# Rotating an 8192 x 8192 float32 array: which outputs of the last but one macro tile go through 32x32 blocks, and who makes their copies

## The chip, the cores and the metric

The kernel runs on one core of a Trainium2 chip. The metric is the device time of one execution in microseconds (us), as the median of several; before the change it is 1263.31 us (three runs, 1263.1 to 1263.37).

## The reference

`reference(x, k)` returns `np.rot90(x, k)` for x of 8192 x 8192 float32 and k = 1: out[8191 - c, r] = x[r, c]. Nothing is calculated; 268.44 MB are read, turned by a quarter, and 268.44 MB are written.

## The kernel before

**Tiles.** x is cut into 16 macro tiles (numbered kk = 0 to 15) of R = 1024 rows by W = 4096 columns. A macro tile is loaded in T = 8 loads of 128 rows each (2 MB; load t of macro tile kk is called kk.t, and has the number m = 8 kk + t) and stored in J = 8 outputs of 512 columns of x each, over all its 1024 rows (2 MB; output j is called kk.j, number n = 8 kk + j). So there are 128 loads and 128 stores, and the 8 outputs of a macro tile need all of its 8 loads. In macro tile 15 alone the outputs are cut otherwise: the first four are halves of two columns of outputs (`END`, `wide`), so that the end does not wait for all rows.

**On-chip buffers.** `bufs` has two landing buffers (LAND) and three output buffers (OUTS); `ring` holds one macro tile less one chunk (SLOTS = T * J - 1). Each load is a row of 8 chunks of 128 x 512. VectorE reads a landed load, reverses each chunk and puts it into its slots of the ring (L337). Macro tiles of even and odd number lay their chunks out crosswise (`slot`), so that load kk.t goes into exactly the slots that output (kk-1).t has been read from. Therefore VectorE waits, ahead of load m = n + 8, until output n has been taken out of the ring.

**Two ways for an output.** `by_pe(kk)` lists the outputs of a macro tile that TensorE turns: it transposes 128x128 pieces into PSUM (L376), and ScalarE copies them out into an output buffer (L415), in three parts. All outputs of macro tiles 0 and 15 go that way; of macro tiles 1 to 13 outputs 0 and 4 (`BY_PE`); of macro tile 14 outputs 0, 4 and 7. The other outputs are *moved*: VectorE puts their chunks into the ring with a STREAM_TRANSPOSE, which turns 32x32 blocks, in place of a plain copy, and afterwards whole quadrants (32 partitions) have to be copied into an output buffer, 16 copies of 32x1024 for an output (`pairs`, `moves`). VectorE makes the first BY_DVE = 2 of them (L319), GpSimd the next BY_POOL = 9 (L294), ScalarE the last 5 (L405).

**Order and waits.** Every engine runs its own list, written out by hand, in order.
- SyncE issues the loads (L256); load m waits (`taken`) until VectorE has put the load two before it, m - 2, wholly into the ring.
- VectorE, for each load m: first its copies for output m - 8 if that is moved; then it waits for load m to land, then for output m - 8 to be out of the ring (`s_pool`, or `s_half` for an output of TensorE), then the pieces of the load.
- GpSimd, for each moved output: it waits for a free output buffer (`room_for`: the store three outputs earlier has landed), and makes 9 copies; ahead of the eighth it waits for ScalarE's copies, ahead of the ninth for VectorE's. So its count says that all 16 copies are done.
- ScalarE, for each output in order: its copies, or the parts out of PSUM; then, for a moved output, the wait for GpSimd's count; then it issues the store (L425). For output 7 it first takes a corner piece out of PSUM (L398).
- TensorE fills two PSUM halves in turn; the third part of an output reuses the half of the first, once ScalarE has emptied it. The last transposition of an output's first part waits for a free output buffer.

`pieces` says in how many instructions VectorE takes a load into the ring; `split` joins chunks that a regular pattern can describe.

Of the kernel before, what the change touches and what calls it, by code (L numbers as in the profile page):

```python
# [13 lines left out]
J = W // (G * P)  # L14
# [5 lines left out]
SLOTS = T * J - 1  # L20

Q = 32
BY_DVE = 2
BY_POOL = 9
BY_PE = [0, 4]

# [33 lines left out]
def kernel(tc: tile.TileContext, x: bass.AP, k: bass.AP, out: bass.AP):  # L60
# [7 lines left out]
    KK = len(macros)  # L68
# [11 lines left out]
    outs = [(*o, [(j, g * P) for j in reversed(o[2]) for g in range(G)]) for o in outs]  # L80

    def by_pe(kk):
        return list(range(J)) if kk in (0, KK - 1) else BY_PE + [J - 1] * (kk == KK - 2)

    def in_quadrants(kk, j):
        return j not in by_pe(kk)
# [29 lines left out]
    with tc.tile_critical():  # L116
# [72 lines left out]
        def split(js):  # L189
            while js:  # L190
                n = max(n for n in range(1, len(js) + 1) if strides(js[:n], 1))
                yield js[:n]
                js = js[n:]
# [3 lines left out]
        for m in range(n_load):  # L197
            kk, t = divmod(m, T)
            here = by_pe(kk)
            rest = [j for j in range(J) if j not in here]  # L200
            if kk == KK - 1:
                got = [here] if t < T - 1 else [here[:wide], here[wide:-1], here[-1:]]
            elif t < T - 1:
                got = [here[: len(BY_PE)], rest, here[len(BY_PE) :]]
                if kk == 0:
                    got = [here]
            else:
                inner = [j for j in here if 0 < j < J - 1]
                got = [here[:1], [J - 1], [j for j in rest if j < J - 1], inner]
            got = [part for js in got for part in split(js)]  # L210
            pieces[m] = got
            for js in got:
                done += 1
                for j in js:
                    rev[m, j] = done
# [16 lines left out]
        def moves(n, share):  # L232
            kk, ts, (j,), _ = outs[n]
            rows = len(ts) * P
            places = [slot(kk, t, j) for t in ts if (t, j) != (T - 1, J - 1)]
            ((step, tiles),) = strides(places, CH)
            for a, q in share:
                yield (
                    at(
                        bufs[out_buf(n)][q * Q : q * Q + Q, :],  # L240
                        a * Q,
                        [[rows, G], [P, tiles], [1, Q]],
                    ),
                    at(
                        ring[a * Q : a * Q + Q, :],
                        places[0] * CH + q * Q,
                        [[P, G], [step, tiles], [1, Q]],
                    ),
                )
# [10 lines left out]
        def turned_in(n):  # L260
            kk, _, (j,), _ = outs[n]
            return rev[kk * T + T - 1 - (j == J - 1), j]
# [7 lines left out]
        with nc.Block() as block:  # L270

            @block.gpsimd
            def _(e):
# [12 lines left out]
                for n, (kk, _, js, _) in enumerate(outs):  # L286
                    if moved[n]:
                        room_for(wait, n)
                        wait(s_rev, turned_in(n))
                        others = {BY_POOL - 2: s_act, BY_POOL - 1: s_dve}  # L290
                        for c, (to, of) in enumerate(moves(n, pairs[BY_DVE : BY_DVE + BY_POOL])):
                            if c in others:
# [16 lines left out]
            def _(e):  # L309
                wait = once(e)  # L310
                for m in range(n_load):
# [3 lines left out]
                    if n >= 0 and moved[n]:  # L315
                        room_for(wait, n)
                        wait(s_rev, turned_in(n))
                        for to, of in moves(n, pairs[:BY_DVE]):
                            i = e.tensor_copy(out=to, in_=of)  # L319
# [66 lines left out]
            def _(e):  # L386
# [3 lines left out]
                for n, (kk, ts, js, blocks) in enumerate(outs):  # L390
# [11 lines left out]
                    if moved[n]:  # L402
                        wait(s_rev, turned_in(n))
                        for to, of in moves(n, pairs[BY_DVE + BY_POOL :]):
                            i = e.copy(to, of)  # L405
# [60 lines left out]
```

## Time and profile before

| What | Value |
|---|---|
| median of three runs | 1263.31 us |
| profiled execution, own time | 1262.84 us |
| its span in the profile | 1261.0 us |
| VectorE busy | 714.8 us, 466 instructions |
| ScalarE busy | 600.8 us, 559 instructions |
| GpSimd busy | 848.2 us, 753 instructions |
| TensorE busy (matmul) | 314.3 us, 1492 instructions |
| HBM traffic | 268.44 MB read, 268.44 MB written |

The profile is of one execution. Times of its rows count from the start of the span; the execution's own time is 1.84 us longer than the span. In the rows PE is TensorE, PEld its weight loads, DVE VectorE, ACT ScalarE, POOL GpSimd, SP SyncE; a small q behind the name marks the queue on which an engine issues transfers. A row names the source line, the operation and what it writes and reads (out<-in), the count, and the time. In brackets stands how long the engine was idle before it, and what ended that idle time. DMA share is the mean busy share of the 16 DMA engines, GB/s what they moved.

### The profile page before, as it was taken

To read this page: it belongs to the slowest core of one execution; us is meant where nothing else is said; L and a number is where in the kernel's file an instruction comes from. 1 tells how busy PE (TensorE), PEld (TensorE's weight loads), DVE (VectorE), ACT (ScalarE), POOL (GpSimd) and SP (SyncE) were. 2 spreads that over 40 slices of the span, in tenths; PEclk is the share of its full clock that TensorE was granted. 3 is DMA by queue.
4 is the path that set the end of the run, shared out by engine and by line. 5 is a ranking of instruction groups with operands and counts; after the bars stand their busy time and mean duration, and the time that the engine had idled before them with its cause. 6 is when DMAs were issued, how large, how long until landed. Compare 5 with 4: busy or idle time off the path is not lost.

```text
span 1261.0 us, 5364 instructions
## 1 busy us (share of the span) xinstructions
PE 314.3 (25%) x1492; PEld 255.1 (20%) x1492; DVE 714.8 (57%) x466; ACT 600.8 (48%) x559; POOL 848.2 (67%) x753
## 2 busy tenths in 40 slices
PE   1555122221122211132202322113221132211273
PEld 1444011211112110121201212012120121201163
DVE  3444765567656666666666665666556665564510
ACT  0344454454445544454445545454454544534564
POOL 0001887778877779777797777877678777788910
PEclk9986555555555555555555555555555555555587
DMA  9999999999999999999999999999999999999999
GB/s 398 417 432 429 427 430 430 428 431 429 428 431 429 429 431 429 429 430 430 428 429 431 429 428 431 429 429 430 428 430 431 429 430 430 429 429 430 388 423 384
DMA packets 36893, 537.21 MB, mean 426 GB/s; under 512 B 4096, under 2 KB 4096, under 8 KB 4096
## 3 DMA queue, kind: packets, MB, share of 16 engines
q10 hardware_dynamic: 18432, 268.44, 50.1%
q1 hardware_dynamic: 18432, 268.44, 49.9%
q8 instruction: 11, 0.18, 0.1%
q14 instruction: 18, 0.15, 0.0%
HBM read 268.44 MB, written 268.44 MB: 426 GB/s over the span
## 4 chain that ended last, share of the span: by engine, by line
DMA 72%; DVE 16%; POOL 5%; ACT 3%; issue 2%; PE 0%; ACTq 0%; SPq 0%; DVEq 0%; POOLq 0%
DMA buf<-in_x_dram 65%; DVE ring L337 16%; DMA out_dram<-buf 7%; POOL buf L294 5%; ACT buf L415 3%; PE ps L376 0%; ACTq L425 0%; DVE buf L319 0%; SPq L256 0%; DVEq L324 0%; SPq L461 0%; POOLq L161 0%; SPq L116 0%
## 5 line engine op out<-in xcount | busy, mean ns | idle before, releaser
L294 POOL COPY buf<-ring 32x1024 f32<-32x1024 f32 (+1 forms) x747 | 847.5, 1135 | 353.9 <-DMA out_dram<-buf 301.1
L405 ACT COPY buf<-ring 32x1024 f32<-32x1024 f32 (+1 forms) x415 | 425.2, 1025 | 314.9 <-POOL buf L294 261.2
L376 PE MATMUL ps<-head,ring 128*128 128x128 f32 x1432 | 301.5, 382 | 927.6 <-DVE ring L337 413.3
L376 PEld LDWEIGHTS ps<-head,ring 128*128 128x128 f32 x1432 | 242.3, 198 | 986.6 <-DVE ring L337 426.3
L337 DVE COPY ring<-buf 128x1024 f32<-128x1024 f32 (+3 forms) x152 | 135.9, 895 | 498.8 <-DMA buf<-in_x_dram 433.2
L337 DVE STREAM_TRANSPOSE ring<-buf 128x3072 f32<-128x3072 f32 (+2 forms) x133 | 367.0, 2771 | 0.0
L415 ACT COPY buf<-ps 128x2048 f32<-128x2048 f32 (+4 forms) x127 | 165.5, 1370 | 241.4 <-PE ps L376 167.4
L319 DVE COPY buf<-ring 32x1024 f32<-32x1024 f32 x166 | 222.4, 1340 | 1.1
L398 ACT COPY buf<-ps 128x512 f32<-128x512 f32 x15 | 8.8, 586 | 86.1 <-POOL buf L294 80.4
L362 PE MATMUL ps<-head,buf 128*128 128x128 f32 x60 | 15.9, 421 | 0.0
L362 PEld LDWEIGHTS ps<-head,buf 128*128 128x128 f32 x60 | 13.1, 230 | 0.0
L332 DVE COPY buf<-buf 128x512 f32<-128x512 f32 x15 | 6.4, 427 | 0.5
L389 ACT ACT_TABLE_LOAD x1 | 1.3, 1283 | 0.9 <-SPq L116 0.9
L274 POOL MEMSET head<- 128x128 f32 x1 | 0.2, 204 | 0.5 <-SPq L116 0.5
L276 POOL TENSOR_SCALAR_AFFINE_SELECT head<-head 128x128 f32<-128x128 f32 x1 | 0.3, 292 | 0.2 <-POOL head L274 0.2
L447 POOL MEMSET const-float32-0.0<- 128x1 f32 x1 | 0.1, 98 | 0.2 <-issue 0.2
L389 ACT COPY head<-head 128x1 f32<-128x1 f32 x1 | 0.2, 192 | 0.0
L447 POOL MEMSET const-uint8-127<- 128x1 uint8 x1 | 0.1, 101 | 0.0
L447 POOL MEMSET const-bfloat16-1.0<- 128x1 bf16 x1 | 0.1, 100 | 0.0
L447 POOL MEMSET const-float32-1.0<- 128x1 f32 x1 | 0.1, 98 | 0.0
## 6 DMA issues: line engine op xcount, KB each, us to landing
buf<-in_x_dram SPq DMA_DIRECT2D x128, 2048.0 KB, 15.4
out_dram<-buf ACTq DMA_DIRECT2D x128, 2048.0 KB, 17.5
```

The costliest lines, as they stand in the source:

```text
L276: e.affine_select(out=ident, in_=ident, compare_op=mybir.AluOpType.not_equal, fill=1.0, base=0, pattern=[[-1, P]], channel_multiplier=1,). ...
L294: i = e.tensor_copy(out=to, in_=of)
L319: i = e.tensor_copy(out=to, in_=of)
L332: e.tensor_copy(out=at(bufs[b][:], 0, [[CH, 1], [1, CH]]), in_=landed(b, js)).then_inc(s_rev, 1)
L337: turn(out=chunk(kk, t, js), in_=landed(b, js)).then_inc(s_rev, 1)
L362: i = e.transpose(corner[:, g * P : g * P + P], bufs[load_buf(m)][:, g * P : g * P + P], ident,)
L376: i = e.transpose(ps[h][:, to : to + P], chunk(kk, t, [j])[:, 0, off : off + P], ident,)
L389: e.copy(scratch, ident[:, :1])
L398: e.copy(at(bufs[b][:], rows - P, [[rows, G], [1, P]]), at(corner, 0, [[P, G], [1, P]]),).then_inc(s_freed, 1)
L405: i = e.copy(to, of)
L415: e.copy(at(bufs[b][:], cols[0], [[rows, deep], [1, run]]), at(ps[h][:], 0, [[run, deep], [1, run]]),).then_inc(s_ev, 1)
L447: nc = _bacc.Bacc("TRN2", target_bir_lowering=False, num_devices=1)
```

## The change

```diff
-BY_DVE = 2
+BY_DVE = 1
 BY_POOL = 9
...
     def by_pe(kk):
-        return list(range(J)) if kk in (0, KK - 1) else BY_PE + [J - 1] * (kk == KK - 2)
+        if kk in (0, KK - 1):
+            return list(range(J))
+        return BY_PE if kk < KK - 2 else [*range(0, J, 2), J - 1]
...
             elif t < T - 1:
-                got = [here[: len(BY_PE)], rest, here[len(BY_PE) :]]
-                if kk == 0:
-                    got = [here]
+                got = [here, rest]
```

First, for every moved output of the whole kernel, VectorE makes one of the 16 quadrant copies instead of two, GpSimd still nine (each shifted by one quadrant pair), ScalarE six instead of five.

Second, in macro tile 14 TensorE turns outputs 0, 2, 4, 6 and 7 (before: 0, 4, 7), and only 1, 3 and 5 are moved (before: 1, 2, 3, 5, 6). So the number of moved outputs falls from 83 to 81.

Third, VectorE takes the loads 14.0 to 14.6 into the ring as a copy of chunks 0, 2, 4, 6, a copy of chunk 7 and a transposition of chunks 1, 3, 5; before it was a copy of 0 and 4, a transposition of 1, 2, 3, one of 5, 6, and a copy of 7. The last load, 14.7, keeps four instructions in the same order of kinds: chunk 0, chunk 7, the transposed ones, and the other plain ones. In the other macro tiles the pieces are the same as before.

## The prediction

> **What bounds the kernel now.** First I read the page: its span and the rate of the transfers in 40 equal slices.
>
> ```profile
> span 1261.0 us, 5364 instructions
> ...
> GB/s 398 417 432 429 427 430 430 428 431 429 428 431 429 429 431 429 429 430 430 428 429 431 429 428 431 429 429 430 428 430 431 429 430 430 429 429 430 388 423 384
> ```
>
> The DMA engines move about 429 GB/s whatever the other engines do. Where that holds, no engine's busy time matters; a change can win only where a slice falls off. Besides the start and the end only the 38th does, with 388. So next the view by windows, cut around that slice (window, length, busy time of PE, PEld, DVE, ACT, POOL with counts, granted clock, DMA share, GB/s).
>
> ```profile
> 180.00:1164.00 984.00, 206.20 (x845) 163.00 (x845) 599.81 (x403) 483.62 (x463) 761.67 (x678) 0.53 1.01 429
> 1164.00:1188.00 24.00, 7.19 (x30) 5.99 (x30) 13.79 (x7) 14.12 (x13) 21.63 (x16) 0.57 0.96 377
> 1188.00:1212.00 24.00, 7.96 (x47) 7.49 (x47) 8.03 (x4) 10.61 (x10) 14.66 (x12) 0.55 1.01 429
> 1212.00:1256.00 44.00, 26.52 (x226) 24.22 (x224) 2.69 (x3) 27.55 (x16) 0.00 (x0) 0.90 1.01 424
> ```
>
> The dip lies between stretches of 429 and costs 24 x (1 - 377/429) = **2.9 us**. The last 44 us are stores alone, at 424. Third, who is late in the dip: the timeline of VectorE, of ScalarE with its queue, and of SyncE's queue.
>
> ```profile
> 1163.87 3.14 DVE L337 COPY ring<-buf 128x4096 f32<-128x4096 f32 x1 [6.37 <-POOL buf L294]
> ...
> 1176.26 2.29 DVE L337 COPY ring<-buf 128x4096 f32<-128x4096 f32 x1 [6.37 <-POOL buf L294]
> ```
>
> ```profile
> 1137.78 0.55 ACTq L425 DMA_DIRECT2D out_dram<-buf  x1
> 1138.88 5.25 ACT L405 COPY buf<-ring 32x1024 f32<-32x1024 f32 x5 [1.13 <-DMA out_dram<-buf]
> 1151.27 0.55 ACTq L425 DMA_DIRECT2D out_dram<-buf  x1
> ...
> 1163.80 0.55 ACTq L425 DMA_DIRECT2D out_dram<-buf  x1
> ...
> 1176.19 0.55 ACTq L425 DMA_DIRECT2D out_dram<-buf  x1
> 1176.78 3.70 ACT L415 COPY buf<-ps 128x2048 f32<-128x2048 f32 x3 [7.13 <-POOL buf L294]
> 1180.51 0.56 ACTq L425 DMA_DIRECT2D out_dram<-buf  x1
> ```
>
> ```profile
> 1145.34 0.33 SPq L256 DMA_DIRECT2D buf<-in_x_dram  x1
> ```
>
> ```profile
> 1154.65 0.33 SPq L256 DMA_DIRECT2D buf<-in_x_dram  x1
> ```
>
> ```profile
> 1167.04 0.33 SPq L256 DMA_DIRECT2D buf<-in_x_dram  x1
> ```
>
> ```profile
> 1178.58 0.33 SPq L256 DMA_DIRECT2D buf<-in_x_dram  x1
> ```
>
> ScalarE's queue issues the stores 14.0 to 14.4 here; the moved ones 14.1, 14.2 and 14.3 come 12.5 and 12.4 us apart, one GpSimd output each. VectorE wants to take in the loads 15.2 and 15.3 and waits 6.37 us each time until GpSimd has finished 14.2 and 14.3; so SyncE's loads 15.4 and 15.5 (the last two rows) go out late. How late is seen from the times to landing, asked for each issue alone; the four loads 15.2 to 15.5, then the stores 14.0, 14.1, 14.2:
>
> ```profile
> DMA to landing us min/median/max: 16.7/16.7/16.7
> ```
>
> ```profile
> DMA to landing us min/median/max: 17.2/17.2/17.2
> ```
>
> ```profile
> DMA to landing us min/median/max: 12.7/12.7/12.7
> ```
>
> ```profile
> DMA to landing us min/median/max: 14.7/14.7/14.7
> ```
>
> ```profile
> DMA to landing us min/median/max: 20.6/20.6/20.6
> ```
>
> ```profile
> DMA to landing us min/median/max: 16.9/16.9/16.9
> ```
>
> ```profile
> DMA to landing us min/median/max: 14.1/14.1/14.1
> ```
>
> Landings are thus 15.2 at 1162.0, 15.3 at 1171.8, 15.4 at 1179.7, 15.5 at 1193.3; stores 14.0 at 1158.4, 14.1 at 1168.2, 14.2 at 1177.9. I call the **lead** of a transfer how long before the landing of its forerunner in the same direction it is issued. Load 15.3: 1162.0 - 1154.65 = 7.4 us; store 14.1: 1158.4 - 1151.27 = 7.1; both before the dip, so both without loss. Load 15.4: 4.8; store 14.2: 4.4; the rate just begins to fall. Load 15.5: 1.1; store 14.3: 1.7; that is the dip: one direction has nothing in flight, and between the landings of 15.4 and 15.5 lie 13.6 us, where a pair of load and store takes 4.194 MB / 429 GB/s = 9.8 us. So a lead of 7 is enough, one of 5 hardly, one of 1 is not.
>
> **The change part by part.** The prices, by shape:
>
> ```profile
> L294 POOL COPY buf<-ring 32x1024 f32<-32x1024 f32 x630 | 725.4, 1151 | 348.8 <-DMA out_dram<-buf 301.1 <-DVE buf L319 23.0
> L405 ACT COPY buf<-ring 32x1024 f32<-32x1024 f32 x350 | 364.5, 1041 | 314.0 <-POOL buf L294 261.2 <-DMA out_dram<-buf 48.8 <-ACT buf L415 0.7
> ...
> L319 DVE COPY buf<-ring 32x1024 f32<-32x1024 f32 x140 | 193.2, 1380 | 0.9
> ...
> L337 DVE COPY ring<-buf 128x1024 f32<-128x1024 f32 x99 | 82.2, 830 | 382.7 <-DMA buf<-in_x_dram 335.4 <-POOL buf L294 44.0 <-PE ps L376 3.3
> ...
> L337 DVE STREAM_TRANSPOSE ring<-buf 128x1536 f32<-128x1536 f32 x21 | 37.2, 1770 | 0.0
> L337 DVE COPY ring<-buf 128x4096 f32<-128x4096 f32 x14 | 34.5, 2462 | 59.5 <-DMA buf<-in_x_dram 41.2 <-POOL buf L294 17.0 <-PE ps L376 1.4
> ...
> L337 DVE STREAM_TRANSPOSE ring<-buf 128x1024 f32<-128x1024 f32 x21 | 25.2, 1201 | 0.0
> ```
>
> *One copy moves from VectorE to ScalarE* in each of 81 moved outputs. VectorE loses 1.38 us an output, ScalarE gains 1.04. Neither stands at the end of an output: GpSimd does, with 9 x 1.15 = 10.4 us against ScalarE's 6 x 1.04 = 6.2. Cost 0, under the cover of GpSimd. What if the cover goes is a rival below. GpSimd itself gets a little faster, as the chain of work shows in output 14.1:
>
> ```profile
> 1143.21 3.00 POOL buf L294
> 1146.25 1.40 POOL buf L294
> ...
> 1149.13 1.03 POOL buf L294
> ```
>
> Its copies take 1.03 us alone, 1.40 beside one of VectorE's quadrant copies (L319), 3.00 beside VectorE's 128x4096 copy. One L319 less is 0.37 us less for GpSimd per output; where GpSimd waits for the second VectorE copy (23.0 us in all in the first row), that goes too. In the 984 us at 429 GB/s this is worth 0, since the transfers are full.
>
> The Trainium skill ("Perfetto Trace Analysis", Optimizing Scalar/DVE Operations) says that a copy which VectorE can do in a performance mode is faster there, and should go to ScalarE only when VectorE is saturated. That speaks against this exchange, with VectorE busy 714.8 of 1261.0 us; the trace disagrees on the price, 1380 ns on VectorE and 1041 on ScalarE for the same shape. By the rule the sum would hold a loss in each output; by the rows it holds none.
>
> *Outputs 14.2 and 14.6 go to TensorE.* GpSimd loses 18 copies in macro tile 14, 20.7 us by the first row. TensorE gains 64 transpositions, ScalarE trades two sets of copies for two sets out of PSUM (3.70 us). *VectorE's intake of loads 14.0 to 14.6*: it loses transpositions of 1536 and 1024 (1.77 + 1.20) for one of 1536; its plain copy of 1024 becomes one of 2048, a shape that the trace lacks: between 0.83 (128x1024) and 2.46 us (128x4096), I take 1.3, being nearer to the smaller. Sum: between -1.20 and +0.43, taken -0.7 us per load. It stands between a load's landing and the issue of the load after next, so a lead grows by 0.7 or shrinks by 0.4: worth 0 at leads of 7.
>
> *Replay of macro tile 14*, with landings 9.8 us apart from the last one that is as before. GpSimd takes for a moved output seven copies of 1.03 with 0.04 between two (1143.21 + 3.00 to 1146.25), one of 3.00 and one of 1.40: 12.0 us (12.4 before). A store of TensorE's follows the one ahead by 4.3 us at least (1176.19 to 1180.51).
> - 14.1 (moved): its buffer comes free at 1138.9 as before, ready 1150.9, lead 7.5.
> - 14.2 (TensorE): ScalarE is free after that issue; 1155.3 in place of 1163.80, lead 12.9 in place of 4.4.
> - Load 15.2 landed at 1162.0; output 14.2 is out of the ring, so VectorE's 6.37 us wait becomes one for the landing. With 2.3 to 3.1 us of copy (the two VectorE rows), load 15.4 goes out at 1164.3 to 1165.1 in place of 1167.04: lead 6.7 to 7.5.
> - 14.3 (moved): buffer of 14.0 free at 1158.4, ready 1170.4 in place of 1176.19; lead on 14.2 (1178.0) 7.6.
> - Load 15.3 at 1171.8 finds 14.3 out; load 15.5 goes out at 1174.1 to 1174.9 in place of 1178.58: lead on 15.4 (now 1181.6) 6.7 to 7.5.
> - 14.4, 14.6 (TensorE) have leads of 13; 14.5 (moved) starts at 1178.0, is ready at 1190.0, lead 7.5 on 1197.5. Loads 15.6 and 15.7 follow as 15.5 does, with the same leads.
>
> No lead is left under 6.7. What is late next is then nothing but the transfers, up to the last load; there the stores 14.6 and 14.7 are still pending, as before, and cover macro tile 15's first outputs. The tail keeps its 44 us at 424.
>
> **Sum:** 1261.0 - 2.9 = 1258.1 us of span. The execution lies 1262.84 - 1261.0 = 1.84 over its span: 1259.9. The median of the runs, 1263.31, lies 0.47 over the profiled one: **1260.4 us**.
>
> **The rivals.**
> 1. *The dip shrinks only.* Leads of 6.7 to 7.5 lie between one that cost nothing (7.1) and one of 4.8, at which the rate fell; VectorE's 128x4096 copies still stretch a GpSimd copy to 3.00. The 2.9 us came with four late transfers (15.4, 15.5, 14.2, 14.3), 0.7 each; if each of the four loads 15.4 to 15.7 still loses half of that, 1.4 us stay: 1261.8. For it: no lead of these has more than 2 us to spare. Against: loads and stores with 7.4 and 7.1 ran at 429.
> 2. *It does not do what it should: the dip is no matter of late issues*, and stays: 1263.3. For it: stores alone run at 424 in the tail, so one direction could carry the whole rate. Against: in the tail several stores are queued, in the dip just one. The Trainium skill ("DMA: Bandwidth & Descriptors", Issuing engines are not separate DMA queues) says that transfers of all queues share the same 16 engines, and the queue of issue saves only issue time; by that rule alone a late load would leave its share to the store and 1263.3 would stand, and the 377 GB/s speak against it.
> 3. *Slower: ScalarE's sixth copy becomes what GpSimd waits for* ahead of its eighth. In the second of two consecutive moved outputs ScalarE starts 0.6 us after GpSimd (it issues the store first) and would end after 0.6 + 6 x 1.04 = 6.9 us; GpSimd's seven copies take 7 x 1.07 = 7.5 uncontended. It decides from 0.6 us more, and shows in the time only where leads fall under 5. At 0.1 us lost in each of the four such outputs of 13 macro tiles, 5.2 us: 1268.5. Against: the margin, and 348.8 us in which GpSimd is idle. The skill's rule on ScalarE above leads here too.
> 4. *More:* the steady stretch also rises by 1 GB/s (984/429 = 2.3 us): 1258.1. Against: it has no visible dip to fill.
>
> **How the numbers follow.** Forecast 0.66, with its own range 1259.7 to 1261.2; rival 1 0.18, rival 2 0.06, rival 3 0.06, rival 4 0.04. The range holds the forecast and rival 1 with 0.2 us beside them: 1259.5 to 1262.0. About 0.2% is what a measurement of this kernel can tell from no change; it ends at 1263.31 x 0.998 = 1260.8, close above the forecast, so of its 0.66 I put 0.56 below and 0.10 above. Faster: 0.56 + 0.04 = 0.60. Within: 0.10 + 0.18 + 0.06 = 0.34. Slower: 0.06.
>
> **What would show it.** Window 1164 to 1188 at 425 or more; VectorE waiting for landings, not GpSimd, at the loads 15.2 and 15.3; SyncE's load 15.5 at about 1174.5; 729 copies on GpSimd, 81 on VectorE's L319 and 486 on ScalarE's L405; the tail of 44 us at 424, ending 2.9 us sooner. The forecast is wrong if the dip stands with early issues (rival 2), if another dip opens, or if GpSimd's idle time shows ScalarE as releaser (rival 3).

## The result, and the profile after

The changed kernel takes **1260.93 us** (median of 16 runs, 1260.7 to 1261.2), the kernel before 1263.25 (16 runs); ratio 0.9982, 95% interval 0.9974 to 0.999. It is 2.3 us faster; forecast were 2.9 us and 1260.4. The profiled execution took 1261.2 us, its span is 1259.3.

From the page of the changed kernel, the span, the rate in 40 slices, and the two groups of quadrant copies of GpSimd and ScalarE:

```profile
span 1259.3 us, 5455 instructions
...
GB/s 398 413 429 431 428 428 430 429 431 429 429 430 429 430 428 429 430 429 431 428 429 432 426 430 429 429 431 428 431 430 428 430 429 429 429 428 429 431 423 372
...
L294 POOL COPY buf<-ring 32x1024 f32<-32x1024 f32 (+1 forms) x729 | 809.1, 1110 | 379.8 <-DMA out_dram<-buf 349.8
L405 ACT COPY buf<-ring 32x1024 f32<-32x1024 f32 (+1 forms) x486 | 497.6, 1024 | 277.8 <-POOL buf L294 178.7
```

The 38th slice, 388 before, is at 431. The view by windows, cut as in the prediction:

```profile
180.00:1164.00 984.00, 212.25 (x877) 168.50 (x877) 519.83 (x319) 562.49 (x540) 742.54 (x671) 0.53 1.01 429
1164.00:1188.00 24.00, 6.95 (x32) 5.91 (x32) 7.21 (x4) 11.35 (x11) 15.94 (x14) 0.64 1.00 427
1188.00:1212.00 24.00, 15.74 (x88) 13.74 (x89) 7.03 (x5) 11.24 (x9) 2.55 (x3) 0.71 1.01 429
1212.00:1256.00 44.00, 25.55 (x215) 23.65 (x213) 0.25 (x1) 25.46 (x14) 0.00 (x0) 0.85 0.99 415
```

The dip is filled (427 in place of 377), and the rate of the steady stretch is unchanged. VectorE's timeline over the loads 15.1 to 15.4:

```profile
1151.69 2.29 DVE L337 COPY ring<-buf 128x4096 f32<-128x4096 f32 x1 [6.37 <-POOL buf L294]
1160.77 2.64 DVE L337 COPY ring<-buf 128x4096 f32<-128x4096 f32 x1 [6.79 <-DMA buf<-in_x_dram]
...
1171.21 2.29 DVE L337 COPY ring<-buf 128x4096 f32<-128x4096 f32 x1 [6.37 <-POOL buf L294]
1180.29 2.64 DVE L337 COPY ring<-buf 128x4096 f32<-128x4096 f32 x1 [6.78 <-DMA buf<-in_x_dram]
```

Every second wait is now for a landing. At 15.3 VectorE still waits for GpSimd, where the prediction had it wait for the landing (1170.5 here), but GpSimd is done with 14.3 at 1171.2 in place of 1176.2. SyncE's two decisive loads, 15.4 and 15.5:

```profile
1163.44 0.33 SPq L256 DMA_DIRECT2D buf<-in_x_dram  x1
```

```profile
1173.54 0.33 SPq L256 DMA_DIRECT2D buf<-in_x_dram  x1
```

The replay had them at 1164.3 to 1165.1 and 1174.1 to 1174.9, and the store 14.3 at 1170.4 (measured 1171.14).

### The profile page after: what moved, and what is told of

It is laid out like the page before. It is cut to its first block, busy times and chain, and to the rows that moved or that the text cites. A ratio compares the mean times of both kernels' runs of the same rounds, so it can differ in the third digit from the quotient of the medians.

```text
span 1259.3 us, 5455 instructions
## 1 busy us (share of the span) xinstructions
PE 326.2 (26%) x1556; PEld 265.3 (21%) x1556; DVE 618.3 (49%) x373; ACT 680.7 (54%) x636; POOL 809.8 (64%) x735
## 4 chain that ended last, share of the span: by engine, by line
DMA 49%; POOL 44%; ACT 3%; issue 2%; DVE 0%; PE 0%; ACTq 0%; POOLq 0%; SPq 0%; DVEq 0%
DMA out_dram<-buf 44%; POOL buf L294 44%; DMA buf<-in_x_dram 4%; ACT buf L415 3%; DVE ring L337 0%; PE ps L376 0%; ACTq L425 0%; POOLq L270 0%; SPq L256 0%; SPq L461 0%; DVEq L324 0%; SPq L118 0%
## 5 line engine op out<-in xcount | busy, mean ns | idle before, releaser
L294 POOL COPY buf<-ring 32x1024 f32<-32x1024 f32 (+1 forms) x729 | 809.1, 1110 | 379.8 <-DMA out_dram<-buf 349.8
L405 ACT COPY buf<-ring 32x1024 f32<-32x1024 f32 (+1 forms) x486 | 497.6, 1024 | 277.8 <-POOL buf L294 178.7
L376 PE MATMUL ps<-head,ring 128*128 128x128 f32 x1496 | 313.4, 381 | 914.1 <-DMA out_dram<-buf 419.2
L376 PEld LDWEIGHTS ps<-head,ring 128*128 128x128 f32 x1496 | 252.5, 198 | 974.8 <-DVE ring L337 430.2
L337 DVE COPY ring<-buf 128x1024 f32<-128x1024 f32 (+5 forms) x152 | 162.0, 1071 | 593.4 <-DMA buf<-in_x_dram 491.3
L337 DVE STREAM_TRANSPOSE ring<-buf 128x3072 f32<-128x3072 f32 (+2 forms) x125 | 357.8, 2871 | 0.0
L415 ACT COPY buf<-ps 128x2048 f32<-128x2048 f32 (+1 forms) x133 | 172.9, 1366 | 218.5 <-PE ps L376 145.4
L319 DVE COPY buf<-ring 32x1024 f32<-32x1024 f32 x81 | 108.1, 1334 | 0.0
## 6 DMA issues: line engine op xcount, KB each, us to landing
buf<-in_x_dram SPq DMA_DIRECT2D x128, 2048.0 KB, 15.3
```

What stands on the lines that cost most here:

```text
L337: turn(out=chunk(kk, t, js), in_=landed(b, js)).then_inc(s_rev, 1)
L376: i = e.transpose(ps[h][:, to : to + P], chunk(kk, t, [j])[:, 0, off : off + P], ident,)
L415: e.copy(at(bufs[b][:], cols[0], [[rows, deep], [1, run]]), at(ps[h][:], 0, [[run, deep], [1, run]]),).then_inc(s_ev, 1)
```

## The experiments

Three theories stood at the start. **A**: GpSimd's queue in macro tile 14 is the whole matter. **B**: the exchange of copies makes the gain. **C**: only the number of moved outputs in macro tile 14 counts. Each time below is a median of 11 runs; the kernel before, on the same chips, took 1263.17 to 1263.34. The intervals of the ratios are about 0.0009 wide to each side; differences between two experiments are read from medians whose runs mostly lie within 0.3 us. In e2 (1261.7 to 1264.3) and e12 (1263.2 to 1265.0) they scatter more.

| Run | What it is | us | ratio to before (95% interval) |
|---|---|---|---|
| e1 | macro tile 14 changed alone | 1261.72 | 0.9986 (0.9978 to 0.9995) |
| e2 | exchange of copies alone | 1262.59 | 0.9994 (0.9985 to 1.0003) |
| e3 | three moved outputs in a row | 1262.22 | 0.9990 (0.9981 to 0.9999) |
| e4 | none moved in macro tile 14 | 1262.30 | 0.9991 (0.9982 to 0.9999) |
| e5 | changed, landed pieces first | 1261.00 | 0.9981 (0.9972 to 0.9990) |
| e6 | e1, landed pieces first | 1261.65 | 0.9986 (0.9977 to 0.9995) |
| e7 | changed, load 15.5 late | 1261.66 | 0.9987 (0.9978 to 0.9995) |
| e8 | changed, ScalarE eight, GpSimd seven | 1262.04 | 0.9990 (0.9981 to 0.9999) |
| e9 | changed, 63 small copies ahead | 1261.07 | 0.9983 (0.9974 to 0.9992) |
| e10 | changed, 90 small copies ahead | 1260.81 | 0.9981 (0.9972 to 0.9990) |
| e11 | e1, 94 small copies ahead | 1261.69 | 0.9988 (0.9979 to 0.9997) |
| e12 | before, 94 small copies ahead | 1263.70 | 1.0004 (0.9996 to 1.0013) |

### Each half alone

```diff
# e1: the changed kernel with
-BY_DVE = 1
+BY_DVE = 2
```

> The changed kernel with VectorE's two copies and ScalarE's five restored: only macro tile 14 is changed. Theory A (GpSimd's queue in macro tile 14 makes loads 15.4 and 15.5 and stores 14.2 and 14.3 late, and nothing else costs): GpSimd needs 12.4 us for an output in place of 12.0, 14.3 is ready at about 1171, load 15.5 goes out before 1175, window 1164 to 1188 at 425 GB/s or more; 1260.9 us, within 0.4. Theory B (the exchange of copies makes the gain, by a faster GpSimd in every macro tile): about 1263.2, the time before. If both parts add: about 1262.

```diff
# e2: the kernel before with
-BY_DVE = 2
+BY_DVE = 1
```

> The kernel before with VectorE's one copy and ScalarE's six: only the exchange of copies. Theory A: GpSimd is 0.4 us quicker per output, three in a row make load 15.5 go out at about 1177.5 in place of 1178.6; the dip stays at 377 to 390 GB/s; 1262.7 to 1263.3. Theory B: 1260.9. Rival 3 of the prediction (ScalarE's sixth copy stops GpSimd in the second of two consecutive moved outputs): above 1264.

The window of the dip, first of e1, then of e2:

```profile
1164.00:1188.00 24.00, 7.78 (x33) 6.58 (x34) 11.76 (x7) 8.91 (x8) 16.41 (x12) 0.50 1.01 428
```

```profile
1164.00:1188.00 24.00, 7.19 (x30) 5.99 (x30) 10.07 (x5) 16.09 (x15) 20.43 (x16) 0.57 0.98 390
```

Macro tile 14 alone fills the dip wholly (428), and yet brings only 1263.34 - 1261.72 = 1.62 us. The exchange alone brings 0.75, with the dip still at 390; its interval includes no change. On top of e1 it brings 1261.72 - 1260.93 = 0.79, and there the runs do not overlap (1261.3 to 1261.9 against 1260.7 to 1261.2). The two add: 1.62 + 0.75 = 2.37, measured for both 2.32. So theory A holds for the dip, but not for the whole gain, and B for a third of it.

### Number or order of the moved outputs

```diff
# the changed kernel with, in by_pe
-[*range(0, J, 2), J - 1]
+[0, 4, 5, 6, J - 1]         # e3
+list(range(J))              # e4
```

> The changed kernel, but in macro tile 14 TensorE turns outputs 0, 4, 5, 6, 7 and the moved ones are 1, 2, 3: as many moved outputs as in the changed kernel, but next to each other. Theory A (what counts is that GpSimd's outputs stand one behind the other): 14.2 ready at about 1163, 14.3 at about 1175, load 15.4 out at 1166, load 15.5 at about 1177.5 with a lead of about 2 us; the dip stays for the most part, 1262.3 to 1263.2. Theory C (what counts is how many outputs GpSimd has in macro tile 14): 1260.9, no dip.

SyncE's loads 15.4 and 15.5, and the window, in e3:

```profile
1166.62 0.33 SPq L256 DMA_DIRECT2D buf<-in_x_dram  x1
```

```profile
1177.80 0.33 SPq L256 DMA_DIRECT2D buf<-in_x_dram  x1
```

```profile
1164.00:1188.00 24.00, 11.04 (x56) 9.77 (x57) 8.62 (x4) 13.65 (x12) 11.04 (x9) 0.58 0.99 390
```

As many moved outputs as in the changed kernel, but the loads go out as late as in e2 (1166.52 and 1177.71 there), the dip stands at 390, and 1.3 us of the time are lost again. It is the order; C falls.

> The changed kernel, but TensorE turns all eight outputs of macro tile 14. Theory A, with leads of 7 us being enough: nothing more to gain, 1260.9 within 0.3, though loads 15.4 to 15.7 go out up to 1 us sooner and stores have leads over 9. Rival 1 of the prediction (leads of 7 still lose a part): 0.3 to 0.6 us faster than the changed kernel, 1260.3 to 1260.6.

e4 is slower than the changed kernel by 1.4 us, which neither side expected. Its window has no dip, but a new loss stands ahead of it:

```profile
1100.00:1164.00 64.00, 25.09 (x138) 21.32 (x137) 22.08 (x12) 34.58 (x33) 33.59 (x27) 0.63 1.00 421
1164.00:1188.00 24.00, 12.50 (x78) 11.15 (x77) 4.62 (x3) 7.59 (x6) 0.00 (x0) 0.86 1.00 428
```

Here 64 x (1 - 421/429) = 1.2 us go. With nothing moved, VectorE takes in the loads of macro tile 14 with 128x4096 copies, and these run beside GpSimd, which is still at the outputs of macro tile 13. Its timeline, and below it GpSimd's part of the chain of work:

```profile
1084.77 3.14 DVE L337 COPY ring<-buf 128x4096 f32<-128x4096 f32 x1 [7.44 <-POOL buf L294]
...
1096.80 2.29 DVE L337 COPY ring<-buf 128x4096 f32<-128x4096 f32 x1 [7.44 <-POOL buf L294]
```

```profile
1072.71 1.03 POOL buf L294
1073.79 3.00 POOL buf L294
1076.83 1.40 POOL buf L294
```

The copy of 3.00 us, which macro tile 14 paid before, has moved ahead to macro tile 13, whose outputs GpSimd still has in rows of two and three. Load 14.5 then leaves 1.8 us ahead of the landing of 14.4, in the changed kernel 4.1. So e4 left the question open whether longer leads bring more.

### The tail, and what the exchange adds

e1 differs from the changed kernel by the exchange alone, and by 0.8 us. What is seen first is a hole in e1's tail. TensorE has done 15.0 early, waits 5.3 us for the last load, and its granted clock is at 0.50 when that lands (window 1212 to 1216); the store 15.1 goes out at 1219.91 (changed kernel 1217.06). So TensorE was made to turn first what has landed:

```diff
+                    if kk == KK - 1 and ts[0] > 0:
+                        order.sort(key=lambda o: ts[o[1] % rows // P] == T - 1)
                     last = dict(order)
```

> The changed kernel, with one order changed in the tail: TensorE turns the pieces of output 15.1 that come from loads 15.4 to 15.6 ahead of those from the last load 15.7 (24 of 32 transpositions ahead of its landing, 8 after). Theory T (since macro tile 14 finishes sooner, TensorE stands idle ahead of the last load, its granted clock falls to 0.5, and output 15.1 comes late into the tail): store 15.1 goes out about 2 us sooner, 0.2 to 0.5 us faster than the changed kernel, 1260.4 to 1260.7. Rival (the tail's loss is the transfers' own): no difference, 1260.9.

> The same order in the tail, on the kernel with macro tile 14 changed alone (1261.72 us, store 15.1 issued 1.9 us after the rate needed it, 389 and 369 GB/s in 1216 to 1224). Theory T: the hole in the tail goes, 0.5 to 0.8 us faster, 1260.9 to 1261.2; so what the exchange of copies adds to macro tile 14 alone is for the most part a matter of the tail. Rival (the exchange adds its 0.8 us through the steady stretch): 1261.7 stays.

The tail of e1, then of e6 (windows of 20 and 22 us):

```profile
1208.00:1228.00 20.00, 14.98 (x105) 14.24 (x106) 2.69 (x3) 10.62 (x6) 0.00 (x0) 0.83 0.98 411
1228.00:1250.00 22.00, 13.62 (x118) 12.51 (x116) 0.00 (x0) 14.94 (x9) 0.00 (x0) 0.96 1.00 422
```

```profile
1208.00:1228.00 20.00, 15.58 (x113) 14.43 (x111) 2.69 (x3) 11.93 (x7) 0.00 (x0) 0.83 1.01 424
1228.00:1250.00 22.00, 11.69 (x101) 10.62 (x99) 0.00 (x0) 13.62 (x8) 0.00 (x0) 0.91 1.00 425
```

In e6 the hole is gone: store 15.1 leaves at 1216.14, 3.8 us sooner, and the window rises from 411 to 424. The time stays: 1261.65 against 1261.72. In e5 it stays as well. Theory T falls in its second half: the hole is real, and costs nothing. Why shows in the last microseconds, where the DMA share falls as the 16 engines run out of work (it counts a packet in the window in which it starts, and so can lie above 1). First the kernel before, then the changed one, then e1, then e6:

```profile
1254.00:1256.00 2.00, 0.00 (x0) 0.00 (x0) 0.00 (x0) 0.00 (x0) 0.00 (x0) 0.50 1.06 451
1256.00:1257.00 1.00, 0.00 (x0) 0.00 (x0) 0.00 (x0) 0.00 (x0) 0.00 (x0) 0.50 0.92 393
1257.00:1259.00 2.00, 0.00 (x0) 0.00 (x0) 0.00 (x0) 0.00 (x0) 0.00 (x0) 0.50 0.43 180
```

```profile
1254.00:1256.00 2.00, 0.00 (x0) 0.00 (x0) 0.00 (x0) 0.00 (x0) 0.00 (x0) 0.50 0.56 238
1256.00:1257.00 1.00, 0.00 (x0) 0.00 (x0) 0.00 (x0) 0.00 (x0) 0.00 (x0) 0.50 0.23 98
1257.00:1259.00 2.00, 0.00 (x0) 0.00 (x0) 0.00 (x0) 0.00 (x0) 0.00 (x0) 0.50 0.00 0
```

```profile
1254.00:1256.00 2.00, 0.00 (x0) 0.00 (x0) 0.00 (x0) 0.00 (x0) 0.00 (x0) 0.50 0.81 344
1256.00:1257.00 1.00, 0.00 (x0) 0.00 (x0) 0.00 (x0) 0.00 (x0) 0.00 (x0) 0.50 0.23 98
1257.00:1259.00 2.00, 0.00 (x0) 0.00 (x0) 0.00 (x0) 0.00 (x0) 0.00 (x0) 0.50 0.02 8
```

```profile
1254.00:1256.00 2.00, 0.00 (x0) 0.00 (x0) 0.00 (x0) 0.00 (x0) 0.00 (x0) 0.50 0.50 213
1256.00:1257.00 1.00, 0.00 (x0) 0.00 (x0) 0.00 (x0) 0.00 (x0) 0.00 (x0) 0.50 0.16 66
1257.00:1259.00 2.00, 0.00 (x0) 0.00 (x0) 0.00 (x0) 0.00 (x0) 0.00 (x0) 0.50 0.02 8
```

Length times share, summed, is the work that a mean engine has left at 1254: 2 x 1.06 + 0.92 + 2 x 0.43 = 3.9 us before, 1.35 in the changed kernel, 1.89 in e1, 1.20 in e6. So e6's mean engine is done 0.7 us sooner than e1's and 0.15 sooner than the changed kernel's; but its last engines work on past 1257 as e1's do, and the last one sets the time.

The kept traces show this directly. For each transfer they hold 16 completions, of which the rows give only the last, as the landing. Those of the very last store, in us:

| Kernel | first | mean | last |
|---|---|---|---|
| before | 1257.99 | 1258.50 | 1259.50 |
| changed | 1254.34 | 1256.02 | 1257.77 |
| e1 | 1255.89 | 1256.59 | 1258.38 |
| e6 | 1253.98 | 1255.82 | 1258.30 |

From e1 to e6 the first completion comes 1.9 us sooner and the last 0.1. In e1 the completions of store 15.0 lie 4.4 us apart, those of 15.1 and all later ones 2.5; in e6 they stay 4.3 apart. So e1's hole held up those that were ahead, and the last one hardly. The Trainium skill ("DMA: Bandwidth & Descriptors", Why a DMA increments its semaphore by 16 and not by 1) has it that a transfer is split over up to 16 engines, which finish independently and each report their own part; these completions agree. Which engine a completion belongs to the traces do not say; below, "the last engine" stands for the last completion.

### One late load

```diff
+                        if m == n_load - 5:
+                            w = 64
+                            for j, c in [(j, c) for j in js for c in range(0, CH, w)]:
+                                i = e.tensor_copy(
+                                    out=at(ring[:], slot(kk, t, j) * CH + c, [[1, w]]),
+                                    in_=at(bufs[b][:], (j + 1) * CH - 1 - c, [[-1, w]]),
+                                )
+                            i.then_inc(s_rev, 1)
+                            continue
```

> The changed kernel, but VectorE takes the one load 15.3 into the ring in 64 small copies in place of one, about 5 us longer, so that load 15.5 goes out at about 1179 as in the kernel before, while all stores keep their leads. Theory A1 (a late transfer costs by its own lead, whichever the direction): 0.7 to 1.1 us, 1261.6 to 1262.0. Theory A2 (the other direction takes over the rate, only loads and stores late together cost): 1261.1 or less.

VectorE's 64 copies took 6.62 us, load 15.5 went out at 1177.52, 4.0 us late against the changed kernel's. The window of the dip stays full:

```profile
1164.00:1188.00 24.00, 8.03 (x34) 6.83 (x35) 11.75 (x67) 10.49 (x10) 15.95 (x14) 0.50 1.00 427
```

So the stores did take over the rate, as A2 had it, and still the kernel lost 0.7 us, as A1 had it. The mean rate did not show the loss. The 63 added instructions could have been the cause by themselves, which the next set answers.

### Fetches of instructions

The list of transfers shows 8 KB transfers of instructions, of which e1, e6 and e7 have one at about 1180 and the changed kernel has none between 1070 and 1255. Small copies at the start, which do nothing but lengthen VectorE's or ScalarE's list, move them.

```diff
+                e.wait_ge(s_id, 2)
+                for c in range(P + 2, P + 2 + 63):      # 90 in e10, 46 in e11 and e12
+                    e.tensor_copy(out=head[:, c : c + 1], in_=ident[:, :1])
                 for m in range(n_load):
...
                 e.copy(scratch, ident[:, :1])
+                for c in range(HEAD - 48, HEAD):        # e11 and e12 alone
+                    e.copy(head[:, c : c + 1], ident[:, :1])
```

> The changed kernel with 63 copies of one column each ahead of everything on VectorE, while it waits for the first load; they only lengthen its list of instructions, so that 8 KB fetches of instructions fall earlier and one more falls at about 1180 us, on the DMA engines, where the changed kernel has none between 1070 and its end. Theory F (a fetch of instructions on one of the 16 DMA engines in the last 100 us makes that engine the last to finish): 0.6 to 0.8 us slower than the changed kernel, 1261.5 to 1261.7, as the run with load 15.5 late. Rival (that run was slower since load 15.5 was late, and what the exchange of copies adds is VectorE's and GpSimd's shorter work): 1260.9.

> The same with 90 copies: the additional fetch falls at about 1120 us, before the last load is issued. If only fetches late in the span matter: 1260.9. If each additional fetch costs, wherever it falls: 1261.5 to 1261.7. If the 63 or 90 copies cost something by themselves at the start, both runs show it alike.

> The kernel with macro tile 14 changed alone (1261.72 us, fetches at 1137 and 1179 us) with 46 such copies on VectorE and 48 on ScalarE at the start, which move its last fetches to about 1050 and 1100 us and add none. Theory F: faster for more instructions, 1260.9 to 1261.2. Rival (the exchange of copies saves by shorter work): 1261.7 or slower.

> The kernel before with the same 46 and 48 copies at the start; its fetches at 1126 and 1180 us move to about 1040 and 1100. Theory F: it gains what the exchange of copies alone gained, 0.6 to 0.8 us, 1262.5 to 1262.7, with the dip as it was. Rival: 1263.3 or slower.

The transfers of instructions between 1070 and 1255, first in the changed kernel, then in e9, then in e1, then in e11 (q14 has the 8 KB ones):

```profile
q8 instruction: 3, 0.05, 0.1%
```

```profile
q8 instruction: 3, 0.05, 0.1%
q14 instruction: 1, 0.01, 0.0%
```

```profile
q8 instruction: 3, 0.05, 0.1%
q14 instruction: 2, 0.02, 0.0%
```

```profile
q8 instruction: 3, 0.05, 0.1%
q14 instruction: 1, 0.01, 0.0%
```

e9 got its late fetch and stayed at 1261.07, and e10 at 1260.81; e11 has one, at 1104, in place of e1's two and stayed at 1261.69; e12 did not gain (1263.70). Theory F falls. With it falls the doubt about e7: as many added instructions and a late fetch cost nothing in e9, so e7's 0.7 us are the late load's.

### ScalarE as the one that is waited for

```diff
# the changed kernel with
-BY_POOL = 9
+BY_POOL = 7
```

> The changed kernel with seven copies on GpSimd and eight on ScalarE for each moved output: ScalarE ends after 0.6 + 8 x 1.04 = 8.9 us, GpSimd's two last copies wait for it, so an output that follows another takes about 11 us in place of 10 in the steady stretch. Rival 3 of the prediction, with its price of 0.1 us for each 0.1 us in 52 outputs: far above 1265. The reading by leads (steady leads of 7 fall to 6, and GpSimd's output in macro tile 14 gets no slower): 1260.9 within 0.4.

GpSimd's two longest waits in e8 (us in total, times, the longest one):

```profile
POOL buf L294 <- DMA out_dram<-buf: 295.3, 29, 119.9
POOL buf L294 <- ACT buf L405: 252.3, 81, 4.2
```

GpSimd waits for ScalarE in all 81 moved outputs, 252.3 us in all, 3.1 each; a part of that stands in place of the two copies that it no longer makes. An output that follows another takes GpSimd 11.05 us on the mean (52 outputs), in the changed kernel 10.17. In macro tile 14, where no output follows another, it takes 10.6 in place of 12.0. The kernel is 1.1 us slower, and not by these waits in the steady stretch: about 1140 us, ahead of macro tile 14's outputs, the last engine is no later than in the other runs with the exchange (the numbers stand in the next section). Where the 1.1 us go after that is not shown.

## Why the prediction was right, and where its terms were not

**What holds.** That transfers bound the kernel, that GpSimd's consecutive outputs in macro tile 14 make the loads 15.4 and 15.5 late and leave the dip, and that placing TensorE's outputs between them fills it: e1 (428), e3 (390 with three in a row) and the changed kernel (427) show it. The issue times of the replay hold within a microsecond.

**The size of the dip.** The step "the dip costs 24 x (1 - 377/429) = 2.9 us" priced the loss by the mean rate of 16 engines. Filling it wholly brought 1.62 us (e1), and, on top of the exchange, 1262.59 - 1260.93 = 1.66, where the mean rate would say 24 x (1 - 390/429) = 2.2. The last engine sets the end, and it lost less in the dip than the mean one. The completions show it: take load 15.2 with store 14.0, which land ahead of the dip, and load 15.6 with store 14.4, which land behind it, and average over each pair. From the first pair to the second the kernel before falls back against e1 by 5.5 us in the first completion, 3.3 in the mean and 1.2 in the last. (The two profiled executions differ by 1.1 us, the medians by 1.6.) The mean rate is not always too high a price: e4's loss ahead of the dip comes to 1.2 us by the rate, and e4 is 1.4 us slower than the changed kernel; e7's late load costs 0.7 us and leaves no mark in the rate at all.

**The exchange, costed at 0.** It is worth 0.75 us alone and 0.79 on top of macro tile 14. The prediction counted on the steady stretch being full, and in its rate nothing can be seen (429 in all). Shown not to be it: the hole in the tail (e6) and the places of the fetches (e9, e11, e12). The completions show where it stands. Averaged over load 15.0 and store 13.6, which land ahead of macro tile 14's outputs, the last completion comes at 1139.8 to 1140.4 us in all nine traces with the exchange, and at 1140.6 to 1141.1 in all five without it; the group means are 0.7 us apart. The first completions and the means of the 16 show no such order. So, by one trace of each kernel, the gain is there before the dip and the tail, and in the last engine alone, which no rate shows. Earlier in the span the same difference goes up and down between 0 and 0.5 us, and the groups overlap. With the exchange GpSimd is quicker (an output that follows another takes 10.2 us in place of 10.6 in the kernel before); how that keeps the last engine nearer to the others is not shown, and stays open.

The landing of the last load goes with the time only in part: in e1, e6, e7, e8 and e11, all between 1261.65 and 1262.04, it comes at 1210.7 to 1211.0, in the changed kernel, e5, e9 and e10, all between 1260.81 and 1261.07, at 1209.4 to 1209.9. But e3, with 1212.4, is faster than e2 with 1211.5, and e4 has 1210.9 at 1262.30.

**The price of a copy.** The prediction weighed the Trainium skill ("Perfetto Trace Analysis", Optimizing Scalar/DVE Operations), by which VectorE is the faster engine where a performance mode is available, and offloading to ScalarE may make sense when VectorE is saturated; it answered that the trace has 1380 ns on VectorE against 1041 on ScalarE. The 1380 ns are VectorE's price beside GpSimd. In e8, where GpSimd is idle more often, 50 of VectorE's quadrant copies run with no GpSimd copy beside them and take 0.57 to 0.64 us; in the kernel before, those with GpSimd copying all along take 1.38 on the mean. So on the price these runs do not speak against the page; they show that here, beside GpSimd, a copy moved off VectorE made the kernel no slower. A smaller term: the copy of 128x2048, taken at 1.3 us, took 1.64 on the mean of 7, so that VectorE's intake grew shorter by 0.4 us by the same sum, not by 0.7.

The two errors, 1.3 us too much for the dip and 0.75 too little for the exchange, went in opposite directions. That the sum came out within 0.5 us is luck.

**"A lead of 7 is enough, one of 5 hardly."** The second half does not hold. The prediction read it off the transfers next to the dip. In the kernel before, nearly all loads from macro tile 3 to 14 have leads of 5.2 to 5.8 us, at 429 GB/s (load 14.0 is issued at 1048.0, and 13.7 lands at 1053.8); in the changed kernel the loads 14.4, 14.5 and 15.0 have 4.0 to 4.1, with 429 in 1100 to 1164. So a lead of 4.8 was no sign of loss. Leads of 1.1 (the dip) and 1.8 (e4) leave a mark in the rate. Load 15.5 in e7 has a lead of about 4 us too, and costs 0.7 us without one; why it costs where those three did not is not shown. "One direction has nothing in flight" was too strong as well: when load 15.5 went out before the change, at 1178.6, the first completion of 15.4 was 2.6 us old and the last still 1.1 ahead, so that some engines had run out of loads and others had not. Whether more than 7 would bring more, e4 was to tell and did not, for its own loss of 1.2 us.

**The rivals.** A shrunken dip (1) did not come: 427. That the dip is no matter of late issues (2) is excluded by e1 and e3. Rival 3 did not come: in the changed kernel GpSimd's waits in these copies are for stores alone (349.8 us), none for ScalarE. Its price was that of the whole delay of 52 outputs; e8 made those 0.9 us longer each, 46 us in all, and lost 1.1 us, none of it shown to come from them. Rival 4 did not come.

**The tail** did not keep its 424: 415 in the same window, since the engines drop out one after the other from 1254 on (424 from 1212 to 1254).

## What to carry to other kernels

Where transfers bound a kernel, look for the slices in which the rate falls, and trace the late issues in them back to the engine whose consecutive long pieces hold up a buffer; spreading the same pieces apart can do what removing them does. Take the price of such a hole by the mean rate for a guess only: the last of the DMA engines sets the end, so a hole costs what that one loses, here some 1.6 of 2.9 us, in the tail of e1 nothing, in e4 about the whole. Longer or shorter waits of an engine off the path can cost nothing that shows (46 us in 52 outputs of e8), and yet an edit that leaves the rate alone can be worth a fraction of a microsecond in the last engine, which no window shows. Read off the steady stretch which lead costs nothing, not off the transfers next to a hole.

## What had not been expected of the hardware

The 16 completions of one store lie up to 8 us apart in the steady stretch (the changed kernel), and 3.4 us apart at its end. A gap in the issue of transfers brings them together again: in the kernel before, store 14.2 completes over 6.8 us, 14.4, behind the dip, over 2.7, and the last over 1.5. GpSimd's 1.03 us copy grows beside VectorE's 128x4096 copy: of 26 meetings of the two in the traces of both kernels, e1, e2, e4 and e8, 25 stretched one copy of GpSimd to between 2.9 and 3.2 us. So taking the 32x32 blocks out of macro tile 14 wholly (e4) made GpSimd slower in macro tile 13.
